# Three weight splits moved ahead of the reordering copies in the first stage of a two-layer decoder trunk, and four of those copies moved from ScalarE to GpSimd

## The chip, the core and the metric

The kernel runs on one core of a Trainium2 chip. Its engines work side by side, each through its own list of instructions in order: TensorE (PE; its weight loads are PEld), VectorE (DVE), ScalarE (ACT), GpSimd (POOL) and SyncE (SP), which here only issues DMAs. The metric is the device time of one execution in microseconds (us), and the median over several runs is compared.

## The reference

A residual stream `h` of 512 tokens by 1024 features goes through two layers. The first layer has a dilated sliding-window attention with three groups of four heads, the second an attention with forget gates over shared keys and values. Each is followed by a gated feed-forward network with a short convolution. Only the start of the first layer matters here:

```python
qkv = xn @ w_qkv
q, k, v = jnp.split(qkv, 3, axis=-1)
q = apply_rope(q.reshape(B, T, A_HEADS, HEAD_DIM), cos, sin)
k = apply_rope(k.reshape(B, T, A_HEADS, HEAD_DIM), cos, sin)
...
for g, (window, r) in enumerate(A_GROUPS):   # ((128, 1), (512, 4), (2048, 16))
    ... # tokens gathered by their residue modulo r, then attention within a band
    o, lse = banded_attention(gather(q), gather(k), gather(v), window // r)
```

Here `xn` is `h` after a root-mean-square norm. For groups 1 and 2 the tokens are needed in another order, by their residue modulo 4.

## The kernel before

**Products in three parts.** Every float32 product of activations and weights is made of three matmuls: both operands are split into a high part (rounded to the matmul's own format) and a low part (the rest), and `mm3` multiplies high by high, high by low and low by high (lines 283, 284 and 285). So each piece of weights, 128 x 1024 elements, must be split before TensorE can use it. ScalarE writes the high part and VectorE the low part.

**Weight pieces.** The class `Weights` holds the pieces in the order of their use. `load` issues their DMAs on SP (line 50). `high` (line 64 where a norm gain is multiplied in, two instructions for a piece of two gain columns) and `low` (line 82, likewise two) split the next piece. `split(n)` splits all pieces up to the n-th, and `get()` hands out the next piece, after it has split up to `ahead - 1` pieces beyond. Before a piece is split, the loads of the two behind it are issued. Pieces 0 to 3 are the queries and keys of group 0, 4 and 5 the values of group 0, 6 to 9 the queries and keys of group 1.

**The first stage, in program order.** The block rows of `h` are transposed by TensorE and split into `xT` (tiles `xah` and `xal`, four 128-row slabs of features in each of two halves `i`, 0 and 1). `qk0(b, ...)` multiplies block `b` with pieces 0 to 3. `qk_post` scales the result on ScalarE (line 1094) and applies the rotary embedding with four GpSimd instructions (lines 1100 to 1103). `reorder` copies `xT` into `xP` (tiles `xph`, `xpl`) with the tokens in the order by residue; it makes one copy for each half `i`, block and part (high or low), 16 in all (line 1083). Blocks 0 and 1 are copied by GpSimd, blocks 2 and 3 by ScalarE. `factors_out` and `factors_in` send the norm factors through DRAM (`rd`) and back in the other order, as DMAs on ScalarE's queue (lines 1065 and 1068). Then `v_proj0` makes the values of group 0 from pieces 4 and 5. Its two calls of `get` also split pieces 6, 7 and 8, since `W.ahead` is 4. In between it transposes the rotated queries and keys (`qk_transpose`, line 1109 on TensorE, line 1112 on VectorE) and makes the scores of blocks 0 and 1 (`scores`, line 1134 on TensorE; `softmax`, line 1119 on VectorE and line 1120 on ScalarE). `wide_proj(1, "qk_ps", ...)` multiplies the reordered `xP` with pieces 6 to 9. Its step `s` uses feature slabs 2s and 2s+1, so steps 0 and 1 read half `i` = 0 of `xP`, steps 2 and 3 half 1.

**Work on the side.** `down_sums` loads rows of the later feed-forward weights (`dsums`, lines 581 to 583 on SP), forms four sums on VectorE (lines 586 to 589) and stores them (line 594 on SP). Each call of `next` on it does one step. `sums` takes two of these row pairs and uses two tiles of the ten-buffer pool `t4` for each, the pool that also holds the raw weight pieces. `down0` uses the pool `t8`.

**The order** on each engine is the program's order; nothing is rescheduled. Semaphores make one engine wait for another. Each hardware DMA takes one of eight semaphores in turn, and waits until the DMA that had it before has landed.

Of the kernel before, what the change touches and what calls it, by code (L numbers as in the profile page):

```python
# [117 lines left out]
def trunk_kernel(ctx, tc, x, norm_gains, w_qkv_a, w_o_a, w_q_b, w_o_b, kv_norm, w_kvf, b_f,  # L118
                 w_up, conv_w, conv_b, w_down, rope, out):
    nc = tc.nc  # L120
    act, dve, pool, pe, sp = nc.scalar, nc.vector, nc.gpsimd, nc.tensor, nc.sync
# [8 lines left out]
    def t8(shape, dt=F32, name="t8"):  # L130
        return p8.tile(shape, dt, tag="t8", name=name)
# [85 lines left out]
    W = Weights(nc, new_raw, lambda: t8([128, 2, 1024], F32R, name="w"), pieces)  # L217
# [849 lines left out]
    def factors_in():  # L1067
        act.dma_start(rt[:, 1], rd.rearrange("(l r) -> l r", r=4))
# [4 lines left out]
    def by_fourth(a, spec="p k (l r) -> p k r l"):  # L1073
        return a.rearrange(spec, r=4)

    def reorder(copy, *blocks):

        for i in range(2):
            for b in blocks:
                for part in range(2):  # L1080
                    src = by_fourth(xT[part][i][:, :, b * 128:b * 128 + 128])
                    dst = xP[part][i].rearrange("p k (r l) -> p k r l", r=4)[:, :, :, b * 32:b * 32 + 32]
                    copy(dst, src.bitcast(F32))
# [6 lines left out]
    def qk_post(g, b, o):  # L1090
        if b == 0:
            qks[g] = t8([128, 4, 8, HD], name=f"qk{g}")
        qk = qks[g][:, b]
        act.activation(qk.rearrange("p a d -> p (a d)"), o, AF.Identity, scale=factor(g, b))
        tu = t2([128, 2, 8, 16], name="tu")
        rb = 4 * min(g, 1) + b
        c2 = rp[:, rb, None, 0:16].to_broadcast([128, 8, 16])
        s_lo = rp[:, rb, None, 16:24].to_broadcast([128, 8, 8])
        s_hi = rp[:, rb, None, 24:32].to_broadcast([128, 8, 8])
        pool.tensor_tensor(tu[:, 0], qk[:, :, 0:16], c2, ALU.mult)  # L1100
        pool.tensor_tensor(tu[:, 1, :, 0:8], qk[:, :, 8:16], s_lo, ALU.mult)
        pool.tensor_tensor(tu[:, 1, :, 8:16], qk[:, :, 0:8], s_hi, ALU.mult)
        pool.tensor_tensor(qk[:, :, 0:16], tu[:, 0], tu[:, 1], ALU.add)
# [224 lines left out]
    rstd0(2)  # L1328
    rstd0(3)
    reorder(pool.tensor_copy, 0, 1)  # L1330
    qk0(2, *range(8))
    qk_post(0, 2, qk_banks[2])
    factors_out()
    qk0(3, *range(8))
    W.ahead = 4
    qk_post(0, 3, qk_banks[3])
    reorder(act.copy, 2, 3)
    factors_in()
    sums = down_sums([(1, 6), (1, 7)], in_two, sp, 1, 3)
    next(sums)  # L1340
# [365 lines left out]
    for n in range(N + 3):  # L1706
        live = n < N
        if live:
            j, i = units[n]
# [91 lines left out]
```

## Time and profile before

| | us |
|---|---|
| time, median of 3 runs | 1112.2 (1111.98 to 1112.93) |
| time of the profiled execution | 1112.3 |
| its span in the profile | 1110.5 |
| TensorE busy | 1099.2 |
| VectorE busy | 875.6 |
| ScalarE busy | 676.9 |
| GpSimd busy | 203.5 |

The span runs from the first to the last instruction that the profiler saw; 1.8 us of the execution's own time lie around it. A matmul of the trace overlaps the next one, so "busy" says that TensorE had work in hand, not that it ran at its peak. In rows of the timeline the first number is the start in us from the span's start, the second the duration of the row, `x6` the number of instructions merged into it, and the bracket the idle time ahead of it with what ended that idle time.

### The profile page before, as it was taken

To read this page: it belongs to the slowest core of one execution; us is meant where nothing else is said; L and a number is where in the kernel's file an instruction comes from. 1 tells how busy PE (TensorE), PEld (TensorE's weight loads), DVE (VectorE), ACT (ScalarE), POOL (GpSimd) and SP (SyncE) were. 2 spreads that over 40 slices of the span, in tenths; PEclk is the share of its full clock that TensorE was granted. 3 is DMA by queue.
4 is the path that set the end of the run, shared out by engine and by line. 5 is a ranking of instruction groups with operands and counts; after the bars stand their busy time and mean duration, and the time that the engine had idled before them with its cause. 6 is when DMAs were issued, how large, how long until landed. Compare 5 with 4: busy or idle time off the path is not lost.

```text
span 1110.5 us, 18087 instructions
## 1 busy us (share of the span) xinstructions
PE 1099.2 (99%) x6609; PEld 951.8 (86%) x6609; DVE 875.6 (79%) x1493; ACT 676.9 (61%) x1120; POOL 203.5 (18%) x305
## 2 busy tenths in 40 slices
PE   9999999999999999999999999999999999999997
PEld 6888889899999988888878788789999999988886
DVE  6597788888788679997686676868887787779894
ACT  7754575756666647576451587756556666747572
POOL 2332001311111211000001455400411111211000
PEclk9999999999999999999999999999999999999999
DMA  9799854468988979793448434593368888989862
GB/s 324 165 360 413 313 178 135 90 181 189 212 192 187 249 248 329 282 326 110 140 145 290 160 102 122 166 286 114 84 179 210 195 186 192 227 268 323 314 246 76
DMA packets 184929, 236.27 MB, mean 213 GB/s; under 512 B 12352, under 2 KB 132152, under 8 KB 184840
## 3 DMA queue, kind: packets, MB, share of 16 engines
q1 hardware_dynamic: 169224, 182.94, 50.8%
q0 software_dynamic: 14944, 52.18, 20.7%
q8 instruction: 52, 0.85, 0.3%
q14 instruction: 37, 0.30, 0.1%
q10 hardware_dynamic: 672, 0.00, 0.0%
HBM read 166.08 MB, written 39.63 MB: 185 GB/s over the span
## 4 chain that ended last, share of the span: by engine, by line
PE 92%; DVE 3%; DMA 2%; issue 1%; ACT 1%; POOL 1%; SPq 0%; DVEq 0%; POOLq 0%; ACTq 0%
PE up L285 12%; PE up L284 12%; PE up L283 12%; PE acc L283 8%; PE acc L284 8%; PE acc L285 8%; PE v_ps L283 2%; PE v_ps L285 2%; PE v_ps L284 2%; PE qk_ps L284 2%; PE qk_ps L285 2%; PE qk_ps L283 2%; PE q_ps L283 1%; PE first L285 1%; PE first L284 1%; PE first L283 1%
## 5 line engine op out<-in xcount | busy, mean ns | idle before, releaser
L283 PE MATMUL acc<-w 128*128 128x512 f32 (+1 forms) x311 | 120.6, 388 | 0.3 <-DVE mix L332 0.3
L285 PE MATMUL acc<-w 128*128 128x512 f32 (+1 forms) x311 | 120.4, 387 | 0.0
L284 PE MATMUL acc<-w 128*128 128x512 f32 (+1 forms) x267 | 103.2, 387 | 0.0
L285 PE MATMUL up<-xsh,w 128*128 128x256 f32 x352 | 99.7, 283 | 0.4 <-DMA w<-wsum 0.4
L78 DVE TENSOR_TENSOR w<-wraw,w 128x1024 fp32r<-128x1024 f32 x62 | 82.1, 1341 | 22.8 <-ACT w L60 20.8
L283 PE MATMUL up<-xsh,w 128*128 128x256 f32 x352 | 99.6, 283 | 0.0
L284 PE MATMUL up<-xsl,w 128*128 128x256 f32 x352 | 99.6, 283 | 0.0
L620 ACT ACTIVATE bb<-up,conv 128x512 f32<-128x512 f32 x80 | 59.7, 776 | 59.5 <-DVE up L1007 48.6
L60 ACT CAST w<-wraw 128x1024 fp32r<-128x1024 f32 x82 | 84.5, 1049 | 18.6 <-DMA wraw<-in_w_up_dram 6.9
L284 PE MATMUL up<-xbl,w 128*128 128x512 f32 (+1 forms) x276 | 93.5, 339 | 0.0
L284 PE MATMUL up<-xcl,w 128*128 128x512 f32 (+1 forms) x276 | 93.5, 339 | 0.0
L283 PE MATMUL up<-xbh,w 128*128 128x512 f32 (+1 forms) x276 | 93.5, 339 | 0.0
L283 PE MATMUL up<-xch,w 128*128 128x512 f32 (+1 forms) x276 | 93.5, 339 | 0.0
L285 PE MATMUL up<-xbh,w 128*128 128x512 f32 (+1 forms) x276 | 93.4, 338 | 0.0
L285 PE MATMUL up<-xch,w 128*128 128x512 f32 (+1 forms) x276 | 93.4, 338 | 0.0
L283 PEld LDWEIGHTS acc<-w 128*128 128x128 f32 x311 | 58.4, 188 | 12.5 <-DVE mix L332 0.7
L285 PEld LDWEIGHTS acc<-w 128*128 128x128 f32 x311 | 58.4, 188 | 11.9
L285 PEld LDWEIGHTS up<-xsh,w 128*128 128x128 f32 x352 | 67.6, 192 | 0.6 <-DMA w<-wsum 0.6
L283 PEld LDWEIGHTS up<-xsh,w 128*128 128x128 f32 x352 | 67.6, 192 | 0.0
L284 PEld LDWEIGHTS up<-xsl,w 128*128 128x128 f32 x352 | 67.6, 192 | 0.0
L621 DVE SCALAR_TENSOR_TENSOR bb<-up,conv,bb 128x511 f32<-128x511 f32 x80 | 59.5, 744 | 5.7 <-ACT bb L620 5.5
L623 DVE SCALAR_TENSOR_TENSOR bb<-up,conv,bb 128x510 f32<-128x510 f32 x80 | 59.9, 749 | 2.8
(312 smaller groups left out, 3147.8 us busy)
## 6 DMA issues: line engine op xcount, KB each, us to landing
wraw<-in_w_up_dram SPq DMA_DIRECT2D x88, 512.0 KB, 5.9
w<-wraw POOLq DMA_DIRECT2D x32, 512.0 KB, 6.4
dT<-dsums SPq DMA_DIRECT2D x28, 512.0 KB, 6.6
w<-wsum POOLq DMA_DIRECT2D x24, 512.0 KB, 5.8
dsums<-in_w_down_dram SPq DMA_DIRECT2D x22, 512.0 KB, 7.4
dsums<-in_w_down_dram SPq DMA_DIRECT2D x44, 256.0 KB, 7.7
hD<-hc POOLq DMA_DIRECT2D x44, 256.0 KB, 7.1
dact<-hD SPq DMA_DIRECT2D x44, 256.0 KB, 5.8
```

The costliest lines, as they stand in the source:

```text
L60: self.nc.scalar.copy(pair[:, 0], raw)
L78: self.nc.vector.tensor_tensor(pair[:, 1], raw, pair[:, 0].bitcast(F32), ALU.subtract)
L283: pe.matmul(o, ah, bh, start=first, stop=False, skip_group_check=shared)
L284: pe.matmul(o, ah, bl, start=False, stop=False, skip_group_check=shared)
L285: pe.matmul(o, al, bh, start=False, stop=last, skip_group_check=shared)
L620: act.activation(bb[:, s, :], ps, AF.Identity, bias=cp[:, 3, ch:ch + 1], scale=cp[:, 2, ch:ch + 1])
L621: dve.scalar_tensor_tensor(bb[:, s, 1:], ps[:, :T - 1], cp[:, 1, ch:ch + 1], bb[:, s, 1:], ALU.mult, ALU.add)
L623: dve.scalar_tensor_tensor(bb[:, s, 2:], ps[:, :T - 2], cp[:, 0, ch:ch + 1], bb[:, s, 2:], ALU.mult, ALU.add)
```

## The change

The function `reorder` gets a parameter `parts` that says which halves `i` it copies. Behind `qk_post(0, 3, ...)` the eight ScalarE copies of blocks 2 and 3 become three steps: four copies (half 1) go to GpSimd, pieces 6, 7 and 8 are split, and the other four copies (half 0) are made by ScalarE as before. The two calls of `get` in `v_proj0` then find these pieces split.

```diff
-    def reorder(copy, *blocks):
+    def reorder(copy, *blocks, parts=(0, 1)):
 
-        for i in range(2):
+        for i in parts:
             for b in blocks:
                 for part in range(2):
                     src = by_fourth(xT[part][i][:, :, b * 128:b * 128 + 128])
...
     qk0(3, *range(8))
     W.ahead = 4
     qk_post(0, 3, qk_banks[3])
-    reorder(act.copy, 2, 3)
+    reorder(pool.tensor_copy, 2, 3, parts=(1,))
+    W.split(9)
+    reorder(act.copy, 2, 3, parts=(0,))
     factors_in()
     sums = down_sums([(1, 6), (1, 7)], in_two, sp, 1, 3)
     next(sums)
```

On each engine the same instructions stand as before, but for the four copies that go from ScalarE's list to GpSimd's. In ScalarE's list the six instructions of line 64 now stand ahead of the copies. On SP the loads of pieces 8, 9 and 10 (six DMAs) now stand ahead of the first three loads of `sums`.

## The prediction

> **What bounds the kernel now.** I read the page's busy times and its chain first, then what TensorE waited for in the first 120 us, and then the timelines of the four engines around the change.
>
> ```profile
> PE 1099.2 (99%) x6609; PEld 951.8 (86%) x6609; DVE 875.6 (79%) x1493; ACT 676.9 (61%) x1120; POOL 203.5 (18%) x305
> PE 92%; DVE 3%; DMA 2%; issue 1%; ACT 1%; POOL 1%; SPq 0%; DVEq 0%; POOLq 0%; ACTq 0%
> PE s_ps L1134 <- DVE qkT L1112: 1.2, 1, 1.2
> PE pT_ps L1156 <- DVE st L1119: 0.3, 1, 0.3
> ```
>
> TensorE is the bound: busy for 1099.2 of 1110.5 us, and 92% of the chain. A change elsewhere pays only where it removes a wait of TensorE. The last two lines are waits from its list of the first 120 us, and both lie behind the change: the scores of blocks 0 and 1 wait for VectorE's copy of the transposed queries and keys, and a later transpose waits for VectorE's softmax to free a PSUM bank. The change should act on these 1.5 us and on what stretches beside them. The engines' timelines show why TensorE waits. ScalarE first:
>
> ```profile
> 33.34 1.14 ACT L1083 CAST xph<-xah 128x512 fp32r<-128x512 f32 x1
> ...
> 40.61 1.18 ACT L1083 CAST xpl<-xal 128x512 fp32r<-128x512 f32 x1
> 41.66 3.82 ACT L64 ACTIVATE w<-wraw,gcol 128x512 fp32r<-128x512 f32 x6
> 45.35 1.57 ACT L1247 ACTIVATE V<-v_ps,rt 128x256 f32<-128x256 f32 x4
> ```
>
> Eight copies fill ScalarE from 33.34 to 41.66, 1.04 us each by their starts. Only then come the six high splits of pieces 6 to 8, 3.69 us to the next row. VectorE follows them:
>
> ```profile
> 24.60 4.49 DVE L82 SCALAR_TENSOR_TENSOR w<-wearly,gcol,w 128x256 fp32r<-128x256 f32 x4
> 42.44 4.06 DVE L82 SCALAR_TENSOR_TENSOR w<-wraw,gcol,w 128x512 fp32r<-128x512 f32 x6 [13.22 <-ACT w L64]
> 46.42 2.48 DVE L1112 COPY qkT<-qkT_ps 128x512 f32<-128x512 f32 x4
> 48.82 0.28 DVE L1119 CUSTOM_DVE_ANT_0 p<-s_ps,mask 128x128 f32<-128x128 f32 x1
> 60.09 0.69 DVE L589 TENSOR_TENSOR dsums<-dsums 128x512 f32<-128x512 f32 x1
> 62.03 0.42 DVE L1119 CUSTOM_DVE_ANT_0 p<-s_ps,mask 128x256 f32<-128x256 f32 x1
> ```
>
> VectorE stands idle for 13.22 us until ScalarE's first split, makes its six low splits until 46.42, and only then copies queries and keys (four copies) and starts the softmax at 48.82. TensorE:
>
> ```profile
> 38.30 1.04 PE L1109 MATMUL qkT_ps<-ident,qk 128*128 128x128 f32 x8
> 44.92 1.03 PE L1109 MATMUL qkT_ps<-ident,qk 128*128 128x128 f32 x8
> 47.16 1.83 PE L1134 MATMUL s_ps<-qkT 64*128 64x128 f32 x16 [1.21 <-DVE qkT L1112]
> 48.92 0.50 PE L283 MATMUL qk_ps<-w,xph 128*128 128x512 f32 x1
> 60.53 2.10 PE L1134 MATMUL s_ps<-qkT 64*128 64x256 f32 x16
> 62.94 1.32 PE L1156 MATMUL pT_ps<-ident,p 128*128 128x128 f32 x8 [0.32 <-DVE st L1119]
> ```
>
> The first two copies' transposes were done at 39.3; their copies come seven microseconds later, because they queue on VectorE behind the low splits, and those behind ScalarE's copies.
>
> **The change part by part.**
>
> *ScalarE.* The six splits start at 33.34, where the copies did, and end at 37.0 (33.34 + 3.69). The four copies left end at 41.2 (4 x 1.04). The first reader of their half of `xP` is the product at 48.92, at the earliest some 47: hidden by 6 us. Line 1247 for its first two blocks comes 4 us earlier, for the other two when TensorE is done with them, as now. The raw pieces must have landed by 33.34:
>
> ```profile
> 18.72 4.65 SPq L50 DMA_DIRECT2D wraw<-in_w_qkv_a_dram x6
> DMA to landing us min/median/max: 4.7/7.7/7.7
> ```
>
> The loads of pieces 8 to 10 were issued by 23.4, and the weights of this stretch land within 7.7 us, so by 31.1. With the change these loads go ahead of the three loads of `sums`, so still earlier; those are used only at 51 and have time. No cost.
>
> *GpSimd.*
>
> ```profile
> 25.01 1.31 POOL L1083 CAST xph<-xah 128x512 fp32r<-128x512 f32 x1
> 36.80 0.47 POOL L1103 TENSOR_TENSOR qk<-tu 128x128 f32<-128x128 f32 x1
> 73.16 0.97 POOL L1100 TENSOR_TENSOR tu<-qk,rope 128x128 f32<-128x128 f32 x1 [35.89 <-ACT qk L1094]
> ```
>
> It is free from 37.3 to 73.2. Four copies at up to 1.31 us end at 42.5. Their half of `xP` is first read in step 2 of `wide_proj`, at about 60: hidden by 17 us. No instruction of GpSimd stands behind them before 73.
>
> *VectorE.* The first low split follows ScalarE by 0.78 us (41.66 to 42.44), so it starts at 34.1, and the six would end at 38.1 at their pace of now. But GpSimd, idle beside them until now, works beside them: on the rotary embedding of blocks 2 and 3, then on the new copies.
>
> ```profile
> L82 DVE SCALAR_TENSOR_TENSOR w<-wraw,gcol,w x10: 743/744/751, 42.4 to 61.4; 128x512 fp32r<-128x512 f32 x10
> L82 DVE SCALAR_TENSOR_TENSOR w<-wearly,gcol,w x8: 485/716/1330, 21.6 to 27.8; 128x256 fp32r<-128x256 f32 x8
> ```
>
> The second line (fewest, median, most ns) has four low splits ahead of GpSimd's copies and the four of the row at 24.60 beside them: at worst a copy adds 1330 - 485 = 845 ns. The rotary embedding ran beside the first four, and even the median is 716. Until 37.3 five splits are through; the sixth and the two copies of queries and keys, beside GpSimd's copies, take at most 0.84 us more each: 38.1 + 0.84 + 2 x (0.62 + 0.84) = 41.9. TensorE asks for the copies at 45.8. The cover is 3.9 us, and I count nothing. The low splits end long before the products that use them.
>
> [...]
>
> *TensorE, the sum.* Eight transposes occupy it for 0.87 us and no longer:
>
> ```profile
> 82.40 0.87 PE qkT_ps L1109 x8
> ```
>
> So it is free at 44.92 + 0.87 = 45.79, and the copies for blocks 0 and 1 are there. Scores of two full blocks take 2.10 us (60.53), 1.05 each; block 0 sees only its own keys, half the width, so I estimate 0.52. The row at 47.16 was stretched as its second block waited for the second copy. The product begins at 45.79 + 0.52 + 1.05 = 47.36, not at 48.92: **1.56 us**.
>
> Next is the wait ahead of 62.94. TensorE arrives at 60.53 + 2.10 = 62.63 now, and at 61.07 after. It needs the softmax of block 2, which starts at 62.03 on VectorE, in a row of work without a gap from 46.42. VectorE's third copy can start at about 45.4, half way through the transposes, the fourth at about 45.95, and the softmax of block 0 at 46.6, that of block 1 when its scores are there, at about 47.7 where it was 49.7. So VectorE comes 1.9 to 2.0 us earlier, the bank is free at 62.94 - 1.9 = 61.04, and the wait of **0.31 us** goes as well. From there on TensorE leads; its products shift together with what they release.
>
> Sum: 1.56 + 0.31 = 1.87 us off the profiled execution's own 1112.3, so 1110.4. That execution is 0.1 above the median of 1112.2; I forecast 1110.3. The bounds for this case: 1.2 us if only the idle time at 47.16 goes, and 2.4 us if the softmax's whole lead and a few tenths of later waits come along: 1109.8 to 1111.0. The median alone wanders by a few tenths of a microsecond.
>
> *SP.* One more thing moves:
>
> ```profile
> 43.88 0.33 SPq L582 DMA_DIRECT2D dsums<-in_w_down_dram x1
> 48.50 0.43 SPq L583 DMA_DIRECT2D dsums<-in_w_down_dram x1
> SPq L582 <- DMA rt<-rd: 3.0, 1, 3.0
> DMA to landing us min/median/max: 5.8/8.7/12.1
> ```
>
> The load at 43.88 waited for the raw buffer of piece 6, which comes free at about 35.5 now. So half a megabyte starts 8 us earlier, ahead of `factors_in`. By the third line a load of `down0` waited 3.0 us until the factors (`rt`) had landed; the one at 48.50 (now next in the turn of semaphores) will. It feeds line 589, at 60.09, some 58.1 after the change. With the median landing of 8.7 us it is there at 57.2: covered by 0.9 us, no cost counted.
>
> **The rivals.**
>
> *Absorbed by the DMAs (no change).*
>
> ```profile
> 63.00:100.00 37.00, 36.94 (x193) 1.00 1.03 397
> ```
>
> Columns: stretch, its length, TensorE busy (instructions), clock, DMA share, GB/s. The DMA engines are full from 63 to 100. If the weights' arrival set the pace there, TensorE would wait for what it gained: 1112.3. Against it: TensorE idles 0.06 us in this stretch, its list has no wait for a DMA there, and weights are split up to three pieces ahead.
>
> *GpSimd and VectorE in turn (smaller gain).* Each of the six low splits waits for a whole GpSimd instruction: four for copies of 1.31, two for rotary steps of 0.5. Then they end at 34.1 + 6 x 0.66 + 4 x 1.31 + 2 x 0.5 = 44.3 to 44.9, with the four copies behind them, until 47.4. The first two are just in time; the softmax starts at 47.4 instead of 46.6, so VectorE leads by 1.4: the gain is 1.4, and the time 1110.8. [...]
>
> *The factors come late (slower).* Place: SP's load behind `rt`. The half megabyte now ahead of the factors can delay them by 0.5 MB at the 303 GB/s of the stretch 41.7 to 48, 1.7 us:
>
> ```profile
> 41.70:48.00 6.30, 5.09 (x47) 4.72 (x47) 5.56 (x9) 6.28 (x12) 0.00 (x0) 1.00 0.85 303
> ```
>
> Issued at 50.2 with the longest landing, 12.1, the load is there at 62.3, and line 589 comes 2.2 us later than before instead of 2 earlier; the splits, the softmax and TensorE follow: 1114.5. It decides once the load lands after 58.1, and turns to a loss after 60.1. Against it: 8.7 is the median, and the turn of semaphores lets the load's first half go early.
>
> That the change does nothing is excluded: the instruction lists show the six splits ahead of the copies.
>
> **How the numbers follow.** Forecast 0.68 (1109.8 to 1111.0), in turn 0.14 (1110.8), absorbed 0.10 (1112.3), late factors 0.08 (1114.5). 0.2%, 2.2 us, is about what a measurement of this kernel can tell from no change; faster by more means under 1110.0. The forecast is 0.3 us short of that: I give it 0.28 of its 0.68. Slower by more is the last rival, 0.08. The rest is 0.64. The range takes in the forecast's bounds and the absorbed case: 1109.6 to 1112.3.
>
> **What would show it.** In the profile after, line 64 on ScalarE starts at 33.3 and line 1083 ends at 41.2; line 82 ends by 40; line 1112 has two copies before 42; TensorE's wait at line 1134 is gone, the first `qk_ps` with `xph` starts at 47.4 and the transpose of 62.94 at 61.1, with no idle time before it. It would be wrong if TensorE's list showed a new wait between 45 and 150, or if VectorE waited for `dsums` before line 589.

## The result, and the profile after

| | before | after |
|---|---|---|
| median, us | 1112.05 (17 runs, 1110.92 to 1113.52) | 1109.76 (17 runs, 1109.29 to 1110.44) |
| ratio to before | 1 | 0.998, 95% interval 0.9972 to 0.9987 |
| profiled execution, us | 1112.3 | 1109.52 |
| its span, us | 1110.5 | 1107.7 |

The changed kernel is 2.29 us faster by the medians; the interval of the ratio makes that 1.4 to 3.1 us. The forecast was 1110.3 us, 0.5 above what was measured.

First the page's busy times and the line of its chain, and then TensorE's waits in the first 130 us (in total, times, longest).

```profile
PE 1098.7 (99%) x6609; PEld 951.8 (86%) x6609; DVE 876.4 (79%) x1493; ACT 674.2 (61%) x1116; POOL 210.0 (19%) x309
PE 96%; DVE 1%; ACT 1%; issue 1%; POOL 1%; DMA 0%; DVEq 0%; SPq 0%; POOLq 0%; ACTq 0%
```

```profile
PE warm L243 <- DVE zero L238: 1.2, 1, 1.2
PE qk_ps L283 <- ACT w L64: 0.4, 1, 0.4
PE qk_ps L284 <- DVE w L82: 0.3, 1, 0.3
PE pT_ps L1156 <- DVE st L1119: 0.2, 1, 0.2
```

Four instructions went from ScalarE to GpSimd (1120 to 1116, 305 to 309). TensorE's list has lost the wait of 1.2 us at line 1134 and the longer of the two at line 1156; no new one has come. The chain is now 96% TensorE. The timelines of ScalarE, VectorE and TensorE show the stage itself:

```profile
33.46 3.79 ACT L64 ACTIVATE w<-wraw,gcol 128x512 fp32r<-128x512 f32 x6
37.15 1.14 ACT L1083 CAST xph<-xah 128x512 fp32r<-128x512 f32 x1
40.27 1.15 ACT L1083 CAST xpl<-xal 128x512 fp32r<-128x512 f32 x1
```

```profile
34.21 5.02 DVE L82 SCALAR_TENSOR_TENSOR w<-wraw,gcol,w 128x512 fp32r<-128x512 f32 x6 [4.89 <-ACT w L64]
39.16 1.27 DVE L1112 COPY qkT<-qkT_ps 128x512 f32<-128x512 f32 x2
45.70 1.29 DVE L1112 COPY qkT<-qkT_ps 128x512 f32<-128x512 f32 x2 [5.26 <-PE qkT_ps L1109]
46.90 0.28 DVE L1119 CUSTOM_DVE_ANT_0 p<-s_ps,mask 128x128 f32<-128x128 f32 x1
58.19 0.69 DVE L589 TENSOR_TENSOR dsums<-dsums 128x512 f32<-128x512 f32 x1
60.41 0.42 DVE L1119 CUSTOM_DVE_ANT_0 p<-s_ps,mask 128x256 f32<-128x256 f32 x1 [0.20 <-PE s_ps L1134]
```

```profile
45.06 1.04 PE L1109 MATMUL qkT_ps<-ident,qk 128*128 128x128 f32 x8
46.03 1.68 PE L1134 MATMUL s_ps<-qkT 64*128 64x128 f32 x16
47.64 0.50 PE L283 MATMUL qk_ps<-w,xph 128*128 128x512 f32 x1
61.33 1.31 PE L1156 MATMUL pT_ps<-ident,p 128*128 128x128 f32 x8
```

VectorE has its low splits behind it at 39.2 and makes the first two copies of queries and keys then, not at 46.4. It now stands idle for 5.26 us until TensorE has the next transposes ready: the order of waiting has turned round. At 60.41 it waits again for TensorE's scores, where before TensorE waited for it. TensorE runs from 45.06 to the row at 61.33 with no bracket of idle time.

This execution reached the stage 0.14 us later than the one before, so the rows are best compared by a length: from the start of the second row of line 1109 to the start of the transposes of line 1156 that stood at 62.94. I call it the stage. Before it took 62.94 - 44.92 = 18.02 us, and after 61.33 - 45.06 = 16.27: **1.75 us less**.

### The profile page after: what moved, and what is told of

The parts are those of the page before. It is cut to its first block, busy times and chain, and to the rows that moved or that the text cites. A ratio compares the mean times of both kernels' runs of the same rounds, so it can differ in the third digit from the quotient of the medians.

```text
span 1107.7 us, 18081 instructions
## 1 busy us (share of the span) xinstructions
PE 1098.7 (99%) x6609; PEld 951.8 (86%) x6609; DVE 876.4 (79%) x1493; ACT 674.2 (61%) x1116; POOL 210.0 (19%) x309
## 4 chain that ended last, share of the span: by engine, by line
PE 96%; DVE 1%; ACT 1%; issue 1%; POOL 1%; DMA 0%; DVEq 0%; SPq 0%; POOLq 0%; ACTq 0%
PE up L284 13%; PE up L283 13%; PE up L285 13%; PE acc L283 8%; PE acc L284 8%; PE acc L285 8%; PE v_ps L283 2%; PE v_ps L285 2%; PE v_ps L284 2%; PE qk_ps L284 2%; PE qk_ps L283 2%; PE qk_ps L285 2%; PE q_ps L283 1%; PE first L285 1%; PE first L283 1%; PE first L284 1%
```

## The experiments

The edits are against the changed kernel, unless said otherwise; "before" in a comparison is the kernel before on the same chip.

**Only the order.** All eight copies stay on ScalarE, behind the splits.

```diff
-    reorder(pool.tensor_copy, 2, 3, parts=(1,))
     W.split(9)
-    reorder(act.copy, 2, 3, parts=(0,))
+    reorder(act.copy, 2, 3)
```

> The three pieces are split ahead of the copies, and ScalarE keeps all eight copies. Theory A (the gain is VectorE's: its copies of queries and keys and its softmax no longer queue behind the low splits; where the reordering copies are made does not matter): the low splits end near 38.5 us, TensorE's wait at line 1134 is gone, the first product with xph starts within 0.3 us of the changed kernel's 47.6, and the time is 1109.5 to 1110.5. Theory B (ScalarE's relief by GpSimd is what counts): ScalarE ends its copies at 45.5, its line 1247 and the first exponentials come some 4 us and 1 us later than in the changed kernel, TensorE waits for them, and at least half of the gain is lost: 1111 or more.

Measured: 1109.97 against 1111.83, ratio 0.9983 (0.9974 to 0.9991). Rows of ScalarE (the DMA issue of `factors_in` on its queue and the last of the eight copies), VectorE and TensorE:

```profile
38.89 0.33 ACTq L1068 DMA_DIRECT2D rt<-rd  x1
44.30 1.14 ACT L1083 CAST xpl<-xal 128x512 fp32r<-128x512 f32 x1
34.05 5.71 DVE L82 SCALAR_TENSOR_TENSOR w<-wraw,gcol,w 128x512 fp32r<-128x512 f32 x6 [4.90 <-ACT w L64]
39.69 1.27 DVE L1112 COPY qkT<-qkT_ps 128x512 f32<-128x512 f32 x2
61.16 1.10 PE L1156 MATMUL pT_ps<-ident,p 128*128 128x128 f32 x6
```

The stage takes 61.16 - 44.89 = 16.27 us, the same to the hundredth. ScalarE's four copies of half 0 end at 41.2, 6 us before the product that reads them at 47.47; its last copy, of half 1, ends at 45.4 and is first read at 62.2. The order alone brings the whole gain; that four copies went to GpSimd is not needed once the splits stand first. The first row shows one thing more: the DMA of line 1068 was issued at 38.89, although it stands behind all eight copies in ScalarE's list and six of them had not started. So here ScalarE's list was taken ahead of its computing, and the DMA at the end of it did its waiting, up to 38.89 us, beside the instructions that are ahead of it.

**Only the copies moved.** GpSimd has its four copies, but the pieces are split where the kernel before split them, in the calls of `get`.

```diff
     reorder(pool.tensor_copy, 2, 3, parts=(1,))
-    W.split(9)
     reorder(act.copy, 2, 3, parts=(0,))
```

> GpSimd makes the four copies, and the three pieces are split behind ScalarE's four copies, as in the kernel before. Theory A: ScalarE starts the splits at 37.6, VectorE's low splits run beside GpSimd's copies from 38.4 to between 42.4 and 45, its first two copies of queries and keys end between 43.7 and 46.3, and TensorE asks for them at 46.0: nearly the whole gain, 1109.7 to 1110.7. Theory C (only the order of the splits counts): no more than a third of the gain, 1111.3 or more. If the low splits and GpSimd's copies shut each other out for whole instructions, VectorE is at the late end and a wait of 0.1 to 0.5 us shows at line 1134.

Measured: 1111.05 against 1111.83, 0.999 (0.9981 to 0.9998), in between the two expectations. ScalarE's splits, the DMA issue of `factors_in` on its queue, VectorE and TensorE:

```profile
39.61 0.33 ACTq L1068 DMA_DIRECT2D rt<-rd  x1
39.99 3.79 ACT L64 ACTIVATE w<-wraw,gcol 128x512 fp32r<-128x512 f32 x6 [1.86 <-DMA rd<-rt]
40.75 4.94 DVE L82 SCALAR_TENSOR_TENSOR w<-wraw,gcol,w 128x512 fp32r<-128x512 f32 x6 [11.04 <-ACT w L64]
45.61 2.47 DVE L1112 COPY qkT<-qkT_ps 128x512 f32<-128x512 f32 x4
62.12 1.10 PE L1156 MATMUL pT_ps<-ident,p 128*128 128x128 f32 x6 [0.32 <-DVE st L1119]
```

ScalarE has done its four copies at 38.1, but does not go on to the splits: its list holds the DMA issue of line 1068 first, which must wait until the factors have been written to DRAM (`rd<-rt`). They have only at 39.6. The splits begin after the idle 1.86 us, the four copies of queries and keys come in one row at 45.61, behind the low splits and 0.19 us after TensorE began the second transposes at 45.42, and the stage takes 62.12 - 45.42 = 16.70 us. Most of the 1.2 us wait is gone, the 0.32 us ahead of line 1156 is not: 1.32 of the 1.75 us.

**Splits last, ahead of the DMA.** The same, but with `W.split(9)` behind ScalarE's four copies and ahead of `factors_in`, so that the DMA holds nothing up.

```diff
     reorder(pool.tensor_copy, 2, 3, parts=(1,))
-    W.split(9)
     reorder(act.copy, 2, 3, parts=(0,))
+    W.split(9)
     factors_in()
```

> As the kernel in which only GpSimd's part was done, but the three splits stand between ScalarE's four copies and the DMA that brings the factors back. There ScalarE stood for 1.86 us ahead of the splits, behind that DMA, which waited for the factors to land in DRAM at 39.6. Theory F (that wait is the gain it lacked): ScalarE starts the splits at 37.6 without idle time, VectorE ends the low splits by 43.5, no wait of TensorE is left at 47 and 63, and the first stage is ahead by the 1.7 to 1.8 us of the changed kernel, 1109.6 to 1110.3. Theory G (GpSimd's copies beside the low splits cost it the rest): TensorE still waits 0.3 us at 62, and the time stays at 1110.6 to 1111.2.

Measured: 1110.68 against 1111.64, 0.9993 (0.9984 to 1.0002), as the second expectation had it; by the medians alone this is not clear of no change, so the reading rests on the rows. VectorE, GpSimd and TensorE:

```profile
38.64 6.78 DVE L82 SCALAR_TENSOR_TENSOR w<-wraw,gcol,w 128x512 fp32r<-128x512 f32 x6 [9.08 <-ACT w L64]
45.34 2.47 DVE L1112 COPY qkT<-qkT_ps 128x512 f32<-128x512 f32 x4
39.75 1.59 POOL L1083 CAST xph<-xah 128x512 fp32r<-128x512 f32 x1
61.86 1.32 PE L1156 MATMUL pT_ps<-ident,p 128*128 128x128 f32 x8 [0.30 <-DVE st L1119]
```

VectorE's first low split comes right behind ScalarE's four copies, which end at 38.0, so ScalarE no longer waits; yet the wait ahead of line 1156 stays. The low splits start 2.1 us earlier than in the experiment above and end only 0.3 earlier, because beside GpSimd's copies six take 6.78 us instead of 4.94. Two of the copies in turn take 1.59 us instead of 1.13. So with GpSimd's copies in this place the whole of the gain needs the splits ahead of ScalarE's copies: there the low splits are done before GpSimd's copies begin. The stage takes 61.86 - 45.28 = 16.58 us.

**The factors' DMA first.**

```diff
+    factors_in()
     reorder(pool.tensor_copy, 2, 3, parts=(1,))
     W.split(9)
     reorder(act.copy, 2, 3, parts=(0,))
-    factors_in()
```

> The changed kernel with the DMA of the returning factors ahead of the splits instead of behind the copies. Theory F: ScalarE's list stands still from 33.4 to 39.5, the splits run until 43.3 and the copies until 47.5, line 1247 comes at 47.5 to 49; VectorE's low splits end near 45.0 and its first two copies near 46.3; TensorE waits for the PSUM bank that line 1247 frees, by 1.5 to 2.5 us, and most or all of the gain is lost: 1111.5 to 1112.8. If ScalarE's list goes on past a DMA that waits: 1109.6 to 1110.3, as the changed kernel.

Measured: 1110.67 against 1111.64, 0.9991 (0.9982 to 1.0): not the loss that I expected. ScalarE and TensorE:

```profile
39.86 0.34 ACTq L1068 DMA_DIRECT2D rt<-rd  x1
40.25 3.79 ACT L64 ACTIVATE w<-wraw,gcol 128x512 fp32r<-128x512 f32 x6 [6.32 <-DMA rd<-rt]
48.08 1.57 ACT L1247 ACTIVATE V<-v_ps,rt 128x256 f32<-128x256 f32 x4
48.98 0.50 PE L283 MATMUL qk_ps<-w,xph 128*128 128x512 f32 x1 [0.73 <-ACT V L1247]
```

The mechanism is there: ScalarE stands still for 6.32 us behind a DMA that can't be issued. The size was wrong. Everything on ScalarE comes late, and TensorE waits 0.73 us for a PSUM bank that line 1247 must empty; but the splits at 40.25 are still 1.4 us earlier than in the kernel before (1.9 against the start of the stage), where eight copies stood ahead of them. The stage takes 62.67 - 45.41 = 17.26 us, 0.76 less than before. With this DMA ahead of ScalarE's work about 1 us of the 1.75 is lost. My prediction didn't list it.

**All sixteen copies on GpSimd.**

```diff
-    reorder(pool.tensor_copy, 2, 3, parts=(1,))
+    reorder(pool.tensor_copy, 2, 3)
     W.split(9)
-    reorder(act.copy, 2, 3, parts=(0,))
```

> All sixteen copies on GpSimd, the three splits ahead on ScalarE, which then makes no copy. Theory A (where the copies are made does not matter, while they are there in time): GpSimd's eight copies run from 40 to 49, half 0 is there at 44.5, the product of blocks 2 and 3 that reads it comes at 50; no wait of TensorE in the stage, 1109.6 to 1110.3. Against it, GpSimd beside VectorE's copies and softmax could stretch these by up to 0.8 us each and bring back the wait at 61: 1110.5 to 1111.5.

Measured: 1110.13 against 1111.64, 0.9986 (0.9978 to 0.9995). GpSimd's last copy and TensorE:

```profile
47.22 1.10 POOL L1083 CAST xpl<-xal 128x512 fp32r<-128x512 f32 x1
61.14 1.32 PE L1156 MATMUL pT_ps<-ident,p 128*128 128x128 f32 x8
```

The stage is 61.14 - 44.87 = 16.27 us again, although the copies run to 48.3; those of half 0, which are read first, end at 44.1. How the eight copies are shared between the two engines decides nothing here, with the splits first.

**How much cover there is.** Additions of 128 x 512 on VectorE, whose result nothing uses, stand between the low splits and the first two copies of queries and keys. Twelve came first, then four and seven, whose expectations take their cost from the twelve:

```diff
     W.split(9)
+    pad = t2([128, 512], name="pad")
+    for _ in range(4):
+        dve.tensor_tensor(pad, h[:, 0, 0:512], h[:, 1, 0:512], ALU.add)
     reorder(act.copy, 2, 3, parts=(0,))
```

> The changed kernel with four of the additions instead of twelve, which took 1.01 us each beside GpSimd's copies. They end at 39.4 + 4.1 = 43.5, the first two copies of queries and keys at 44.8, 1.2 us ahead of TensorE: no wait at line 1134, the stretch from the second transposes (line 1109) to the transposes of line 1156 stays at 16.3 us, and the time is that of the changed kernel within 0.4 us, 1109.6 to 1110.4. If VectorE's work costs TensorE anything while it is covered, it is longer by some of the 4.1 us.

> Seven additions: VectorE is free at 39.4 + 7.1 = 46.5, as in the kernel before (46.4). TensorE waits 1.1 to 1.3 us at line 1134 and about 0.3 us ahead of line 1156, the stretch from the second transposes to these is 18.0 to 18.3 us as in the kernel before, and its clock stays at 1.00, so the time is 1111.4 to 1112.3: the gain given back by VectorE alone, with the changed order on ScalarE and GpSimd in place. If twelve cost so much for another reason than the wait (the additions themselves, or GpSimd slowed by them), seven cost 7/12 of 8.5 us, 5 us: 1115.

> The changed kernel with twelve additions of 128 x 512 (two inputs in SBUF, 0.69 us each when alone, result unused) on VectorE between the low splits and the copies of queries and keys, to see how much the cover of VectorE there holds: it stood idle for 5.3 us. Twelve take 8.0 us by the pace of line 588, up to 9.5 beside GpSimd's copies: 2.7 to 4.2 us more than the cover, so TensorE's wait at line 1134 comes back with 2.5 to 4 us, and the time is 1112.2 to 1114. If VectorE is not what TensorE waited for, nothing changes: 1109.6 to 1110.3.

Measured: 1110.42 with four (0.9988, 0.9978 to 0.9997), 1113.87 with seven (1.0017, 1.0008 to 1.0027), both against 1111.87, and 1118.58 with twelve against 1111.64 (1.0061, 1.0046 to 1.0076). VectorE's rows with four, then VectorE's, GpSimd's and TensorE's with seven:

```profile
40.41 4.75 DVE L1341 TENSOR_TENSOR pad<-h 128x512 f32<-128x512 f32 x4
45.08 1.27 DVE L1112 COPY qkT<-qkT_ps 128x512 f32<-128x512 f32 x2
46.92 1.29 DVE L1112 COPY qkT<-qkT_ps 128x512 f32<-128x512 f32 x2 [0.57 <-PE qkT_ps L1109]
```

```profile
40.04 8.55 DVE L1341 TENSOR_TENSOR pad<-h 128x512 f32<-128x512 f32 x7
41.12 1.59 POOL L1083 CAST xph<-xah 128x512 fp32r<-128x512 f32 x1
49.24 1.83 PE L1134 MATMUL s_ps<-qkT 64*128 64x128 f32 x16 [2.28 <-DVE qkT L1112]
65.03 1.32 PE L1156 MATMUL pT_ps<-ident,p 128*128 128x128 f32 x8 [0.33 <-DVE st L1119]
```

Four eat 4.7 of VectorE's 5.26 idle us, and 0.57 is left; the stage is still 62.55 - 46.28 = 16.27 us. So the cover is real, and about 5 us wide. With seven it is gone, and both of the old waits are back, the first one longer than before: the stage takes 65.03 - 45.93 = 19.10 us. Both the wait and the time came out above what I expected (1.1 to 1.3 us and at most 1112.3). I had counted an addition at 1.01 us, the mean of the twelve, which ran in part after GpSimd's copies had ended. The seven run beside them until shortly before their end and take 8.55 us, 1.2 each. The median is 2.0 us above before, the stage only 1.08; the interval (0.9 to 3.0 us) holds both. In the profiled execution the rest lies ahead of the stage, which it reached at 45.93 instead of 44.92: TensorE waited 0.56 and 0.29 us more for its first weights at about 10 us, long before the additions. Whether the other executions had that too isn't recorded.

Twelve lose more than TensorE's wait for VectorE, and both the wait and the time are far above what I expected of them (2.5 to 4 us, 1112.2 to 1114), since I had counted 8.0 to 9.5 us for all twelve and they took 12.18. TensorE's row and the windows of the same stretch (length, then busy time and instructions of PE, PEld, DVE, ACT and POOL, granted TensorE clock, DMA share, GB/s):

```profile
52.30 3.10 PE L1134 MATMUL s_ps<-qkT 64*128 64x128 f32 x16 [5.91 <-DVE qkT L1112]
```

```profile
46.40:52.30 5.90, 0.00 (x1) 0.00 (x1) 5.70 (x9) 1.28 (x1) 0.34 (x1) 0.89 0.82 269
52.30:55.40 3.10, 3.10 (x17) 2.45 (x17) 2.60 (x12) 1.12 (x6) 0.00 (x0) 0.50 0.88 308
55.40:58.00 2.60, 2.60 (x7) 2.08 (x8) 2.57 (x10) 2.60 (x13) 0.00 (x0) 0.53 0.39 150
58.00:60.00 2.00, 2.00 (x10) 1.66 (x9) 1.93 (x4) 1.15 (x2) 0.00 (x0) 1.00 0.00 0
```

The wait is 5.91 us, and the stage 70.16 - 45.35 = 24.81, 8.54 more than after the change. Most of the other 2.6 us comes from the clock. It is 0.50 in the second window and 1.00 in the last. If it went from 1.00 to 0.50 in one step and back in one, the means of 0.89 and 0.53 put the first step, by my estimate, some 1.3 us before the end of the wait and the second at some 57.9, after about 5.6 us of work. The scores take 3.10 us, against 1.83 in the kernel before, where they followed VectorE's copies in the same way; the rest of the slow stretch costs about as much again: the six products behind the scores take 2.65 us by their starts, the next six 1.36. After the 2.28 us wait with seven additions the clock stayed at 1.00.

**The same two kernels again.** The stage explains 1.75 us, the medians differ by 2.29 and the two profiled executions by 2.8. Is there a second gain elsewhere?

> The changed kernel once more, for a second profile of the stretches around 389 and 715 us, where its first profile gained 0.6 and 0.5 us beyond the first stage. Theory D (these two belong to single executions): the waits there differ from profile to profile, also between two executions of one kernel. Theory E (they belong to the change): both stay away in every execution of the changed kernel and stand in every one of the kernel before. The median is 1109.4 to 1110.1 by both.

> The kernel before once more, for a second profile of the stretches around 389 and 715 us. Theory D: the waits there (0.4 us for a DMA into w, 0.4 us of the scores for VectorE) are not both of the same size as in the first profile. Theory E: both stand as they were. The waits at 47 (1.2 us) and 63 us (0.3 us) stand as they were by both.

Measured: 1110.03 for the changed kernel against 1111.83 (0.9983, 0.9974 to 0.9992), so 1.80 us less; one execution of the kernel before at 1112.29. Three waits of TensorE far behind the stage, from its list over the whole span: two of the first profile of before, and one of the experiment with the order alone.

```profile
PE up L285 <- DMA w<-wsum: 0.4, 1, 0.4
PE s_ps L1628 <- DVE nm L1638: 0.4, 1, 0.4
```

```profile
PE up L285 <- DMA w<-wsum: 0.8, 1, 0.8
```

The changed kernel's profiles have neither of the first two, which accounts for 0.63 us at 389 us and 0.54 at 715 when the 6609 matmuls of the two first profiles are matched one by one. But the second profile of before has neither of the two, and the kernel with the order alone, which has the whole gain in the stage, waits 0.8 us at line 285. These waits come and go between executions. The stage repeats: 63.27 - 45.25 = 18.02 us in the second profile of before and 61.64 - 45.37 = 16.27 in that of after, the length that three of the experiments have too. I read the gain as 1.75 us, and the rest of the 2.29 as chance that both intervals leave room for.

## Why the prediction was right

*TensorE's wait for the copies: forecast 1.56 us, measured 1.42.* The first product with `xph` came 47.64 - 45.06 = 2.58 us into the stage, before 48.92 - 44.92 = 4.00. The mechanism was as written. The 0.14 between the two are small errors of the sum: the scores began 0.97 us after the transposes did, not 0.87, and from their start to the product it took 47.64 - 46.03 = 1.61 us, not 0.52 + 1.05 = 1.57.

*The wait ahead of line 1156: forecast 0.31, measured 0.33.* The stage shrank by 1.75, of which 1.42 are above. The reason given, VectorE's lead on the softmax, held: it started at 46.90 instead of 48.82, and at block 2 waited 0.20 us itself. Moving only the copies shortened VectorE's lead, and this wait came back.

*The sum: forecast 1.87, measured 1.75* in the stage, and 2.29 (1.4 to 3.1) by the medians, with 1.80 in the repetition.

*ScalarE: right, with a gap.* Splits at 33.46, copies done by 41.4 (forecast 41.2). That a DMA stood in ScalarE's list behind the copies, and must wait until 39.6, was not looked at. In both kernels that wait passes beside copies or splits that stand ahead of it; the two experiments with the splits behind it lost 0.43 and 0.99 us of the 1.75. Of the 0.43, 0.31 was still lost with the splits ahead of the DMA, beside GpSimd's copies.

*GpSimd: the end was off by 1.8 us, harmlessly.* I had the last copy end at 42.5; it ended at 44.3. Two rows of its timeline after, a step of the rotary embedding and the first copy:

```profile
34.70 0.78 POOL L1101 TENSOR_TENSOR tu<-qk,rope 128x64 f32<-128x64 f32 x1
39.90 1.14 POOL L1083 CAST xph<-xah 128x512 fp32r<-128x512 f32 x1
```

The rotary steps of 0.32 us took up to 0.78 beside the low splits, so the copies began at 39.90 and not at 37.3. Their first reader, the first product of step 2, comes at 62.40 (I had put it at about 60), so the cover is 18 us.

*VectorE: the copies had the room that was counted.* The low splits took 5.02 us instead of 4.06. I had taken the rotary steps as harmless and the copies as the trouble; it was the reverse, since the delayed copies began after the last low split. The first two copies of queries and keys ended at 40.4 (bound 41.9), and the four additions show that 4.7 us more would still be free.

*SP: as forecast.* Its list of issues has line 582 at 36.06 us (forecast some 35.5). The wait behind the factors, by SP's list of waits:

```profile
SPq L583 <- DMA rt<-rd: 3.7, 1, 3.7
```

It held a load of `down0`'s second row pair, issued at 48.59, and VectorE's line 589 at 58.19 didn't wait for it.

*The rivals.* Absorbed by the DMAs fell: from 63 to 100 us TensorE was busy all the time, with the DMA engines as full as before.

```profile
63.00:100.00 37.00, 37.00 (x191) 30.95 (x190) 32.38 (x62) 18.95 (x48) 10.11 (x16) 1.00 1.04 404
```

GpSimd and VectorE in turn is half true: they do hold each other up. In the kernel before, three low splits of 128 x 256 beside GpSimd's copies of 1.29 to 1.31 us took 1.31 to 1.33 us each, one to a copy, where the shortest of that size took 0.49; and the row of 6.78 us shows it for these very splits, which took 4.06 with GpSimd idle. But here the low splits were through at 39.2 instead of 44.3, and the copies began at 39.90, so the splits and the copies did not run at the same time. Late factors fell with SP's row.

The chances leaned to "within 0.2%" since the forecast lay 0.3 us short of that line; the medians came out a hair beyond it (0.21%). In the repetition of the same change the gain was 1.80 us (0.16%), so on which side of that line the medians fall is chance; the 1.75 us of the stage are 0.16%. That the forecast of 1110.3 lay only 0.5 us off the median says little: in the stage the sum was 0.12 us too large, while the medians gave 0.42 us more than it.

## What to carry to other kernels

When the bounding engine waits for a small step on another engine, look at what stands ahead of that step in that engine's list and who waits for each item: here four copies of 0.6 us stood behind six splits, and those behind eight copies, of which the first was read seven microseconds after the last had ended. Putting the order right was enough. Moving work to an idle engine brought part of the gain by itself (1.32 and 1.44 us of the stage), added nothing to the right order, and in the old order brought contention of its own (six low splits in 6.78 us instead of 4.06). Look also for DMA issues in the list of a computing engine: here one that couldn't be issued yet kept ScalarE idle for 6.32 us, so work that could run meanwhile belongs ahead of it.

## What the runs showed of the hardware

- The clock after a wait: with 2.28 us of waiting (seven additions) TensorE's granted clock stayed at 1.00. With 5.91 us (twelve) it was at 0.50 when work went on; by my estimate from the windows' means it fell some 4.6 us into the wait and stayed at half for 5.6 us of work, which cost about 2.5 us on top of the wait.
- GpSimd and VectorE side by side on 128 x 512 float32: a GpSimd copy went from 1.13 to 1.59 us, six low splits from 4.06 to as much as 6.78, an addition on VectorE from 0.7 to 1.2 (the mean of seven).
- A DMA issue in ScalarE's list stopped the work behind it for 6.32 us, but not the copies ahead of it: in the kernel with the order alone it went out while six of these had yet to start.
- That DMA waited for one of 2 KB, issued at 29.34 us in the kernel before, that had landed only at about 39.5, by the issue of line 1068 at 39.74. Around it the DMA engines moved next to nothing while they counted as busy; the window of the changed kernel:

```profile
33.50:41.70 8.20, 8.20 (x71) 8.20 (x70) 6.22 (x8) 8.20 (x13) 8.04 (x11) 1.00 0.82 27
```

27 GB/s at a DMA share of 0.82. The DMA of 2 KB has 528 packets in the trace (queue q10 between 29 and 41 us), so about four bytes each; whether that is the cause was not tried, and stays open.
